# First two chunks loaded, squared, scaled and transposed in halves on two queues, with products of zeros on TensorE until they come

## The chip, the cores and the metric

The kernel runs on one core of a Trainium2 chip. The metric is the device time of one execution in microseconds (us). Five engines run their own instruction queues in order: TensorE (PE; its weight loads are shown as PEld), VectorE (DVE), ScalarE (ACT), GpSimd (POOL) and SyncE (SP). DMAs are issued from SP's queue and from ACT's queue; in the profile they are DMA queues q1 (SP) and q10 (ACT).

## What is computed

The reference is one step of a two-layer decoder trunk: a retention layer and a sliding-window attention layer, over a prompt of 1024 tokens and 8 single decode tokens. Only the start of the first layer matters here:

```
h = rmsnorm(x, g_norm)          # x: 1024 prompt rows and 8 decode rows, 1024 wide
proj = h @ w_in                 # q, k, v, gate
```

where rmsnorm multiplies each row by the inverse root of its mean square (plus 1e-6) and by the gain g_norm. All of it is float32. The kernel forms a product in three passes of rounded float32 (type fp32r): high part times high part, high times low and low times high, where the low part is what the rounding left over.

## The kernel before

The prompt is cut in 8 chunks of 128 rows; chunk 8 stands for the 8 decode rows. For each chunk c there are these steps:

- `xload(c)` issues the load of the chunk (512 KB, 32 KB for chunk 8) on SP's queue.
- `sq(c)` squares it on ACT and sums each row (one Square over 1024 columns, then a read of the accumulator); `pw(c)` makes the factor out of the sum with two small instructions on GpSimd; `sc(c)` multiplies the rows by the factor and the gain `gb` on VectorE.
- `TR(c, b)` transposes the chunk on TensorE in 8 blocks of 128x128, into two PSUM banks; `hi(c, j)` and `lo(c, j)` take the high part (ACT) and the low part (VectorE) of half j out of them. `dcols` puts the columns of the decode rows beside those of the chunks: in the tile of 258 columns, 256 come from two chunks and 2 from the decode rows, so that a product of the first kind needs chunks 0 and 2 and columns of chunk 8.

The weights come in raw tiles of 512 KB (`raw_load`); `w_hi` takes a high part on ACT, `w_lo` a low part on GpSimd or VectorE. The first two weight sets (q0 and k0, head 0) are multiplied in 16 plain slots of 24 products (`plain`, line 556); the work of the other engines in these slots is written out by hand in a list `ops`, and a planner orders everything after them by due times. All queues are in order, so the order in which the program writes instructions of an engine is the order in which the engine takes them.

The start is written out by hand too, at lines 771 to 806: two loads on ACT's queue (the gain `gb`, broadcast to 128 partitions, and the identity `ident`), the table load with a dummy Silu, then on SP's queue chunks 8, 0, 2, two raw tiles of q0, chunks 1 and 3, two raw tiles of k0, chunks 4, 6 and 7. Then

```
    for c in (8, 0, 2):
        sq(c)
        pw(c)
    sc(8)
    ...
    sc(0)
    TR(0, 1)
    dve.tensor_copy(rdec, p8)
    sc(2)
    TR(2, 2)
```

where the lines left out transpose the 8 decode rows into `p8` (8 small transposes on TensorE). After it come `dcols`, `hi`, `lo`, and the high and low parts of the first two weight quarters, A11 and A12.

Of the kernel before, what the change touches and what calls it, by code (L numbers as in the profile page):

```python
# [7 lines left out]
F32 = mybir.dt.float32  # L8
F32R = mybir.dt.float32r
AF = mybir.ActivationFunctionType  # L10
# [4 lines left out]
D = 1024  # L15
# [10 lines left out]
EPS = 1e-6  # L26
# [37 lines left out]
def trunk(tc, x_prompt, x_sample, state_ret, cache_k, cache_v, norm_ret, w_in_ret, ret_out_norm,  # L64
          w_out_ret, norm_swa, w_in_swa, q_norm, k_norm, sinks, w_out_swa, c1, c2,
          y_p, y_s, nrp, nrs, nkp, nvp, nks, nvs):
    nc = tc.nc
    ctx = ExitStack()
    with ctx:
        ctx.enter_context(tc.manual_schedule(engines=MS))  # L70
        _trunk(ctx, tc, nc, locals())


def _trunk(ctx, tc, nc, a):
    x_prompt, x_sample, state_ret = a["x_prompt"], a["x_sample"], a["state_ret"]
# [19 lines left out]
    mm = nc.tensor.matmul  # L95
# [6 lines left out]
    def tr(out, in_, ident, start=True, stop=True):  # L102
        nc.tensor.matmul(out, in_, ident, is_transpose=True, start=start, stop=stop)  # L103
# [13 lines left out]
    def rsq(out, in_, n):  # L117
        nc.gpsimd.tensor_tensor(out, in_, mhalf[:in_.shape[0], :n], ALU.pow)
# [21 lines left out]
    sp = su.enter_context(tc.tile_pool(name="sp", bufs=1, reuse_waits="tile"))  # L140

    xdecr = dcp.tile([128, 8, 40], F32R, name="xdecr")
    xdecd = dcp.tile([128, 4, 40], F32R, name="xdecd")
    oneh_r = dcp.tile([128, 8, 8], F32R, name="oneh_r")
    warm = dcp.tile([1, 8], F32, name="warm")
# [14 lines left out]
    def bank(i, t):  # L160
        return abp.tile([128, 512], F32, tag=f"b{i}{t}", name=f"b{i}{t}")
# [6 lines left out]
    ADD, SUB, MUL = ALU.add, ALU.subtract, ALU.mult  # L168
    act, dve, pool = nc.scalar.activation, nc.vector, nc.gpsimd
# [5 lines left out]
    def raw_tile():  # L175
        return wq.tile([128, 1024], F32, tag="raw", bufs=5, name="raw")

    def raw_load(s, r, eng):

        sub, j = r // 2, r % 2  # L180
        kk = 512 // s.fw
        t = raw_tile().rearrange("p (k f) -> p k f", k=kk)
        r0 = 512 * j + 256 * sub
        eng.dma_start(out=t, in_=w_in_ret[r0:r0 + 128 * kk, s.c0:s.c0 + 2 * s.fw].rearrange("(k p) f -> p k f", p=128))
        s.raw.append(t)
# [224 lines left out]
    gb = sp.tile([128, D], F32, name="gb")  # L410
# [4 lines left out]
    rdif = sp.tile([128, 4, ND], F32, name="rdif")  # L415
    junk = xq.tile([128, D], F32, name="junk")
    X, SS, PO = {}, {}, {}

    def xload(c):
        if c in (0, 1, 2, 3):  # L420
            X[c] = xq.tile([128, D], F32, tag="xq", bufs=4, name="xq")
        elif c == 7:
            X[c] = raw_tile()
        else:
            X[c] = sp.tile([128, D], F32, tag="u", bufs=3, name="u")
        if c == 8:
            X[c] = X[c][0:ND, :]
        nc.sync.dma_start(out=X[c], in_=x_sample[:, 0, :] if c == 8 else x_prompt[0, c * 128:c * 128 + 128, :])

    def sq(c):  # L430
        SS[c] = sp.tile([128, 1], F32, name="ss", bufs=4)
        n = X[c].shape[0]
        act(junk[:n], X[c], AF.Square, accum_out=SS[c][:n])

    def pw(c):
        n = X[c].shape[0]
        pool.tensor_scalar(SS[c][:n], SS[c][:n], 1.0 / D, EPS, MUL, ADD)
        rsq(SS[c][:n], SS[c][:n], 1)

    def sc(c):  # L440
        n = X[c].shape[0]
        dve.scalar_tensor_tensor(X[c], X[c], SS[c][:n], gb[:n], MUL, MUL)

    def TR(c, b):

        PO[c] = [bank(b, j).rearrange("p (k t) -> p k t", k=4) for j in range(2)]
        for j in range(2):
            for k in range(4):
                tr(PO[c][j][:, k, :], X[c][:, 512 * j + k * 128:512 * j + k * 128 + 128], ident)

# [40 lines left out]
    def dcols(t, x, src=None):  # L491

        if src is None:
            k0, r0 = DB[x]
            src = rdec[:, k0:k0 + 4, r0 + 2 * t:r0 + 2 * t + 2]
        h = XH[t][x][:, :, 256:258]
        dve.tensor_copy(h, src)
        dve.tensor_tensor(XL[t][x][:, :, 256:258], src, h.bitcast(F32), SUB)
# [81 lines left out]
    def prod_slot(s, j, t):  # L580
# [14 lines left out]
        if j >= 3:  # L595
# [10 lines left out]
    ops = [  # L606
        [o(w_hi, q0, "A21", 0), o(w_hi, q0, "A22", 0), o(keep, 0, 0), o(keep, 0, 1), o(w_lo, q0, "A21", 0, pool),
         o(w_lo, q0, "A22", 0), o(xload, 5), o(sq, 1), o(pw, 1)],
        [o(sq, 3), o(pw, 3), o(w_hi, k0, "A11", 0), o(w_hi, k0, "A12", 0), o(sc, 1), o(keep, 2, 0), o(keep, 2, 1),
         o(w_lo, k0, "A11", 0, pool), o(w_lo, k0, "A12", 0)],  # L610
        [o(hi, 1, 0), o(hi, 1, 1), o(w_hi, k0, "A21", 0), o(w_hi, k0, "A22", 0), o(sc, 3), o(dcols, 0, T3), o(lo, 1, 0),
         o(lo, 1, 1), o(w_lo, k0, "A21", 0, pool), o(w_lo, k0, "A22", 0)],
        [o(hi, 3, 0), o(hi, 3, 1), o(sq, 4), o(t12, 1), o(dcols, 0, B22), o(lo, 3, 0), o(lo, 3, 1), o(pw, 4), o(t34, 1)],
        [o(sq, 6), o(th, T2, 1), o(t12, 3), o(sc, 4), o(pw, 6), o(t34, 3), o(rsums)],
        [o(th, T2, 3), o(th, T1, 1), o(sc, 6), o(dcols, 1, B11), o(dcols, 1, B21), o(tl, T2, 1), o(tl, T2, 3)],
        [o(hi, 4, 0), o(hi, 4, 1), o(lo, 4, 0), o(lo, 4, 1), o(sq, 5), o(pw, 5), o(keep, 4, 0), o(keep, 4, 1),
# [14 lines left out]
    n = 0  # L631
# [32 lines left out]
    for s in sets[2:]:  # L664
# [31 lines left out]
        for r in range(2 * s.subs):  # L696
            free = raws[-5] + 1.6
            need = min(reads[r])
            t = max(free, need - 13.0)
            t = raw_t[0] = max(t, raw_t[0] + 0.01)  # L700
# [4 lines left out]
        if v:  # L705
            n = len(slots)
# [64 lines left out]
    dve.memset(warm, 0.0)  # L771
    pool.memset(xdecr.bitcast(F32), 0.0)
    pool.memset(xdecd.bitcast(F32), 0.0)
    nc.scalar.dma_start(out=gb, in_=norm_ret[0].partition_broadcast(128))
    nc.scalar.dma_start(out=ident, in_=a["c1"][:, 0:128])
    act(warm, warm, AF.Silu)
    for c in (8, 0, 2):
        xload(c)
    for r in range(2):
        raw_load(q0, r, nc.sync)  # L780
    for c in (1, 3):
        xload(c)
    for r in range(2):
        raw_load(k0, r, nc.sync)
    for c in (4, 6, 7):
        xload(c)
    for c in (8, 0, 2):
        sq(c)
        pw(c)
    sc(8)  # L790
    p8 = vdp.tile([128, 8, ND], F32, tag="vd", name="pd8")
    for k in range(8):
        tr(p8[:, k, :], X[8][:, k * 128:k * 128 + 128], ident[:ND, :ND])
    sc(0)
    TR(0, 1)
    dve.tensor_copy(rdec, p8)
    sc(2)
    TR(2, 2)
    dcols(0, B11)
    dcols(0, B21)  # L800
    for c, name in ((0, "A11"), (2, "A12")):
# [6 lines left out]
    for n, s in enumerate(slots):  # L808
        while pes and pes[0][0] <= s.t:
            _, fn, args = pes.pop(0)  # L810
# [7 lines left out]
        while ev and ev[0][0] < end:  # L818
            _, _, fn, args = ev.pop(0)
# [25 lines left out]
    def o_view(half):  # L845

        if half:
            return B_hi, B_lo, B_hif
        return [t.rearrange("p a b -> p (a b)").rearrange("p (k t) -> p k t", k=16) for t in (A_hi, A_lo, A_hif)]
# [291 lines left out]
    O_hi, O_lo, _ = o_view(0)  # L1141
# [550 lines left out]
    def so_all():  # L1692
        order = [(ft, ti) for ti in range(3) for ft in range(6)] + [(ft, ti) for ft in (6, 7) for ti in range(3)]
        early = []

        def start(ft, ti):
            so_ahead(ft // 2 + 1)
            t0, t1 = TG[ti]
            n = t1 - t0
            xr = iop2.tile([128, 384], F32, tag="xr", bufs=2, name="xr2")  # L1700
            nc.sync.dma_start(out=xr[:, :n], in_=xscr[ft, :, t0:t1])
            nso[0] += 1
            ps = (msp.tile([128, 512], F32, tag="ms", name="pm") if nso[0] % 3 == 0 else
                  pjp.tile([128, 512], F32, tag="pj", name="pj"))
            for k in range(7):
                proj(ps[:, :n], so_slots[ft // 2], ft % 2, t0, t1, first=(k == 0), last=False, ks=[k])
                yield 3 * n / 2400.0
            early.append((ft, ti, ps, xr))

        def finish():  # L1710
            ft, ti, ps, xr = early.pop(0)
            t0, t1 = TG[ti]
            n = t1 - t0
            proj(ps[:, :n], so_slots[ft // 2], ft % 2, t0, t1, first=False, last=True, ks=[7])
            yield 3 * n / 2400.0
            yt = io("sq", 2)
            nc.vector.tensor_tensor(yt[:, :n], ps[:, :n], xr[:, :n], ALU.add)
            if pend_y:
                so_y(*pend_y.pop(0))
            pend_y.append((ft, ti, yt))  # L1720

        for ft, ti in order:
            while early and (oready[early[0][1]] or len(early) == 3):
                while not oready[early[0][1]]:
                    yield 1e9
                yield from finish()
            while ti == 2 and not oready[2]:
                yield 1e9
            yield from start(ft, ti)
        while early:  # L1730
            yield from finish()
        while pend_y:
            so_y(*pend_y.pop(0))
# [43 lines left out]
    out = so_all()  # L1777
# [85 lines left out]
```

## Time and profile before

| | |
|---|---|
| median of 3 runs | 1357.28 us (1355.23 to 1359.15) |
| the profiled execution's own time | 1359.16 us |
| its span, first to last instruction | 1357.4 us |
| mean granted clock of TensorE | 0.989 |
| TensorE busy | 1313.8 us, 97% of the span |
| GpSimd, VectorE, ACT busy | 56%, 55%, 49% |

Times inside the trace are counted from the span's start. A line such as L442 is the source line of the kernel; many steps share a helper's line, so the tile's name tells them apart: u is chunk 8 here (and later chunks), xq are chunks 0 to 3, ss the row sums, xh and xl the high and low parts of chunks, woh and wol those of weights, raw the weight tiles, pd the transposed decode rows, b the PSUM banks. In rows of instructions the first number is the start, the second the time to the end of the last of the merged instructions, and brackets hold the idle time of the engine before it and what ended it. The granted clock (PEclk) is a share of 2.4 GHz.

### The profile page before, as it was taken

What the parts mean: (1) busy time and instruction counts of PE and PEld (TensorE: products, weight loads), DVE (VectorE), ACT (ScalarE), POOL (GpSimd) and SP (SyncE); (2) the same over time, 40 slices, a digit from 0 to 9 for tenths busy, and PEclk for the clock granted to TensorE, in tenths of its full rate; (3) what the DMA queues carried; (4) which work ended last, traced back from release to release, by engine and by line L of the source; (5) the groups of instructions that cost most, each with busy time, mean ns of one, the idle gap of its engine ahead of it and who ended that gap; (6) DMA issues with size and microseconds to landing.
All of it is one profiled execution on the core that took longest, in us unless ns stands there. A gap on an engine that the chain in (4) does not pass through costs nothing.

```text
span 1357.4 us, 25979 instructions
## 1 busy us (share of the span) xinstructions
PE 1313.8 (97%) x9541; PEld 1252.9 (92%) x9541; DVE 744.6 (55%) x1436; ACT 670.8 (49%) x1692; POOL 759.8 (56%) x886
## 2 busy tenths in 40 slices
PE   6999999999999999898989999999999999999998
PEld 6999999999999999787868889988999999998998
DVE  6943665656565653577762112334567777779321
ACT  5532555555565663576751111244576766667311
POOL 6753656656566663698976554563376666544000
PEclk9999999999999999999999999998999999999999
DMA  6314767677676762556546444451111111113533
GB/s 220 103 55 141 216 206 238 164 236 231 183 236 187 229 180 63 194 179 208 173 149 185 145 144 125 142 169 55 32 49 46 48 44 47 34 34 97 166 83 81
DMA packets 193859, 187.19 MB, mean 138 GB/s; under 512 B 12756, under 2 KB 173580, under 8 KB 193716
## 3 DMA queue, kind: packets, MB, share of 16 engines
q1 hardware_dynamic: 156832, 148.34, 35.8%
q10 hardware_dynamic: 36900, 37.19, 8.6%
q8 instruction: 75, 1.23, 0.4%
q14 instruction: 52, 0.43, 0.1%
HBM read 129.11 MB, written 57.41 MB: 137 GB/s over the span
## 4 chain that ended last, share of the span: by engine, by line
PE 84%; DVE 6%; POOL 3%; ACT 3%; DMA 2%; issue 2%; ACTq 0%; SPq 0%; POOLq 0%; DVEq 0%
PE b L340 7%; PE b L342 7%; PE b L341 7%; PE pj L1111 5%; PE pj L1112 5%; PE pj L1113 5%; PE pj L1160 4%; PE pj L1161 4%; PE pj L1162 4%; PE b L334 4%; PE b L333 4%; PE b L335 4%; PE tr L103 4%; PE S L922 1%; PE S L923 1%
## 5 line engine op out<-in xcount | busy, mean ns | idle before, releaser
L340 PE MATMUL b<-xh,woh 128*128 128x258 f32 x784 | 222.4, 284 | 0.0
L342 PE MATMUL b<-xh,wol 128*128 128x258 f32 x784 | 221.9, 283 | 0.0
L341 PE MATMUL b<-xl,woh 128*128 128x258 f32 x784 | 221.6, 283 | 0.0
L1111 PE MATMUL pj<-A_hi,wh 128*128 128x384 f32 (+1 forms) x512 | 173.0, 338 | 1.9 <-ACT Qd L1416 1.9
L1113 PE MATMUL pj<-A_hi,wl 128*128 128x384 f32 (+1 forms) x512 | 166.2, 325 | 0.0
L1112 PE MATMUL pj<-A_lo,wh 128*128 128x384 f32 (+1 forms) x512 | 166.2, 325 | 0.0
L1101 POOL TENSOR_TENSOR wl<-wr,wh 128x512 fp32r<-128x512 f32 (+1 forms) x68 | 124.6, 1844 | 50.5 <-DVE wh L1100 21.2
L340 PEld LDWEIGHTS b<-xh,woh 128*128 128x128 f32 x784 | 148.2, 189 | 1.2
L341 PEld LDWEIGHTS b<-xl,woh 128*128 128x128 f32 x784 | 148.8, 190 | 0.0
L342 PEld LDWEIGHTS b<-xh,wol 128*128 128x128 f32 x784 | 148.2, 189 | 0.0
L334 PE MATMUL b<-wol,xh 128*128 128x256 f32 x448 | 126.1, 282 | 1.2 <-DVE wol L224 1.2
L333 PE MATMUL b<-woh,xh 128*128 128x256 f32 x448 | 125.9, 281 | 0.0
L335 PE MATMUL b<-woh,xl 128*128 128x256 f32 x448 | 125.8, 281 | 0.0
L1527 POOL TENSOR_TENSOR s<-s,sm 128x512 f32<-128x512 f32 x64 | 67.6, 1058 | 76.5 <-DVE sm L1526 71.4
L282 POOL TENSOR_TENSOR yl<-yd,yh 128x256 fp32r<-128x256 f32 x64 | 56.3, 880 | 82.6 <-PE od L289 39.0
L1111 PEld LDWEIGHTS pj<-A_hi,wh 128*128 128x128 f32 x512 | 98.0, 191 | 2.4 <-ACT Qd L1416 2.2
L1112 PEld LDWEIGHTS pj<-A_lo,wh 128*128 128x128 f32 x512 | 98.0, 191 | 0.0
L1113 PEld LDWEIGHTS pj<-A_hi,wl 128*128 128x128 f32 x512 | 97.8, 191 | 0.0
L224 POOL TENSOR_TENSOR wol<-raw,woh 128x512 fp32r<-128x512 f32 x52 | 68.8, 1330 | 48.0 <-ACT woh L219 47.2
L334 PEld LDWEIGHTS b<-wol,xh 128*128 128x128 f32 x448 | 84.4, 188 | 1.4 <-DVE wol L224 1.4
L333 PEld LDWEIGHTS b<-woh,xh 128*128 128x128 f32 x448 | 84.4, 188 | 0.7
L335 PEld LDWEIGHTS b<-woh,xl 128*128 128x128 f32 x448 | 84.4, 188 | 0.0
(384 smaller groups left out, 3836.4 us busy)
## 6 DMA issues: line engine op xcount, KB each, us to landing
raw<-in_w_in_ret_dram ACTq DMA_DIRECT2D x44, 512.0 KB
st<-in_state_ret_dram SPq DMA_DIRECT2D x64, 256.0 KB
out_dram<-st SPq DMA_DIRECT2D x64, 256.0 KB
wr<-in_w_out_ret_dram SPq DMA_DIRECT2D x32, 512.0 KB
wr<-in_w_in_swa_dram SPq DMA_DIRECT2D x18, 512.0 KB
vb<-vscr SPq DMA_DIRECT2D x64, 128.0 KB
evp<-qks SPq DMA_DIRECT2D x32, 256.0 KB
evw<-gsc SPq DMA_DIRECT2D x32, 256.0 KB
```

The lines of the kernel that those rows point to most:

```text
L224: eng.tensor_tensor(lo, src_of(s, name, sub), hi.bitcast(F32), SUB)
L333: mm(dst, xh, wh, start=a and i == 0, stop=False, skip_group_check=True)
L334: mm(dst, xh, wl, start=False, stop=False, skip_group_check=True)
L335: mm(dst, xl, wh, start=False, stop=z, skip_group_check=True)
L340: mm(dst, wh, xh, start=a, stop=False, **sg)
L341: mm(dst, wh, xl, start=False, stop=False, **sg)
L342: mm(dst, wl, xh, start=False, stop=z, **sg)
L1101: lo_eng[0].tensor_tensor(lo[:, js, :], raw[:, i:i + step, :], hi.bitcast(F32)[:, js, :], ALU.subtract)
L1111: mm(ps, hi[:, k, fs], xh[:, k, t0:t1], start=first and k == ks[0], stop=False)
L1112: mm(ps, hi[:, k, fs], xl[:, k, t0:t1], start=False, stop=False)
L1113: mm(ps, lo[:, k, fs], xh[:, k, t0:t1], start=False, stop=last and k == ks[-1])
L1527: nc.gpsimd.tensor_tensor(st[:, :, 0:256], st[:, :, 0:256], sm.unsqueeze(2).broadcast_to([128, 2, 256]), ALU.mult)
```

## The change

On SP and ACT both: chunks 0 and 2 are loaded in two halves of 512 columns, one on each queue, ahead of all else; chunk 8 is loaded behind chunks 0 and 2 and the two raw tiles of q0. Squares of chunks 0 and 2 are taken by halves with a scaled input, so that their sums add up to the mean; their scalings are split in halves too, each followed by its four transposes. The order of Squares is 0, 2, 8 instead of 8, 0, 2, and that of scalings 0, 8, 2 instead of 8, 0, 2. The dummy Silu with its table load stands behind the DMA issues. 34 products of a zeroed tile with itself, of 320 columns, are put ahead on TensorE; their result in bank (0, 0) is never read.

```
     def xload(c):
...
-        nc.sync.dma_start(out=X[c], in_=x_sample[:, 0, :] if c == 8 else x_prompt[0, c * 128:c * 128 + 128, :])
+        if c in FIRST:
+            for j in range(2):
+                js = slice(512 * j, 512 * j + 512)
+                (nc.sync, nc.scalar)[j].dma_start(out=X[c][:, js], in_=x_prompt[0, c * 128:c * 128 + 128, js])
+        else:
+            nc.sync.dma_start(out=X[c], in_=x_sample[:, 0, :] if c == 8 else x_prompt[0, c * 128:c * 128 + 128, :])
 
     def sq(c):
-        SS[c] = sp.tile([128, 1], F32, name="ss", bufs=4)
+        SS[c] = sp.tile([128, 2], F32, name="ss", bufs=4)
         n = X[c].shape[0]
-        act(junk[:n], X[c], AF.Square, accum_out=SS[c][:n])
+        if c in FIRST:
+            for j in range(2):
+                js = slice(512 * j, 512 * j + 512)
+                act(junk[:, js], X[c][:, js], AF.Square, scale=D ** -0.5, accum_out=SS[c][:, j:j + 1])
+        else:
+            act(junk[:n], X[c], AF.Square, accum_out=SS[c][:n, 0:1])
 
     def pw(c):
         n = X[c].shape[0]
-        pool.tensor_scalar(SS[c][:n], SS[c][:n], 1.0 / D, EPS, MUL, ADD)
-        rsq(SS[c][:n], SS[c][:n], 1)
+        r_ = SS[c][:n, 0:1]
+        if c in FIRST:
+            pool.tensor_scalar(r_, r_, SS[c][:, 1:2], EPS, ADD, ADD)
+        else:
+            pool.tensor_scalar(r_, r_, 1.0 / D, EPS, MUL, ADD)
+        rsq(r_, r_, 1)
...
+    def scTR(c, b):
         for j in range(2):
+            xj = X[c][:, 512 * j:512 * j + 512]
+            dve.scalar_tensor_tensor(xj, xj, SS[c][:, 0:1], gb[:, 512 * j:512 * j + 512], MUL, MUL)
+            TR(c, b, (j,))
+
+    def TR(c, b, js=(0, 1)):
+        if 0 in js:
+            PO[c] = [bank(b, j).rearrange("p (k t) -> p k t", k=4) for j in range(2)]
+        for j in js:
             for k in range(4):
                 tr(PO[c][j][:, k, :], X[c][:, 512 * j + k * 128:512 * j + k * 128 + 128], ident)
...
+    xload(0)
     nc.scalar.dma_start(out=gb, in_=norm_ret[0].partition_broadcast(128))
     nc.scalar.dma_start(out=ident, in_=a["c1"][:, 0:128])
-    act(warm, warm, AF.Silu)
-    for c in (8, 0, 2):
-        xload(c)
+    xload(2)
     for r in range(2):
         raw_load(q0, r, nc.sync)
-    for c in (1, 3):
+    for c in (8, 1, 3):
         xload(c)
     for r in range(2):
         raw_load(k0, r, nc.sync)
     for c in (4, 6, 7):
         xload(c)
-    for c in (8, 0, 2):
+    act(warm, warm, AF.Silu)
+
+    zb = bank(0, 0)
+    for _ in range(34):
+        mm(zb[0:40, 0:320], xdecr[:, 0, :], xdecr.rearrange("p a b -> p (a b)"), start=True, stop=True)
+    for c in (0, 2, 8):
         sq(c)
         pw(c)
+    scTR(0, 1)
     sc(8)
     p8 = vdp.tile([128, 8, ND], F32, tag="vd", name="pd8")
     for k in range(8):
         tr(p8[:, k, :], X[8][:, k * 128:k * 128 + 128], ident[:ND, :ND])
-    sc(0)
-    TR(0, 1)
+    scTR(2, 2)
     dve.tensor_copy(rdec, p8)
-    sc(2)
-    TR(2, 2)
     dcols(0, B11)
     dcols(0, B21)
```

## Rows read from the trace of the kernel before

**Rows 1.** The page, busy time and share of the span of each engine.
```profile
PE 1313.8 (97%) x9541; PEld 1252.9 (92%) x9541; DVE 744.6 (55%) x1436; ACT 670.8 (49%) x1692; POOL 759.8 (56%) x886
```
**Rows 2.** Waits, 0 to 45 us: engine, line, waited for, us in total, times, longest.
```profile
PE b L556 <- POOL wol L224: 1.5, 1, 1.5
```
**Rows 3.** Chain that ended last, 0 to 60 us: start, length, what.
```profile
1.19 5.50 DMA xq<-in_x_prompt_dram
...
15.43 3.79 POOL wol L224 x3
...
25.63 1.72 PE b L556 x12
```
**Rows 4.** A stretch: length; PE, PEld, DVE, ACT, POOL busy; clock, DMA, GB/s.
```profile
100.00:545.00 445.00, 445.00 (x3726) 440.38 (x3725) 249.22 (x418) 229.38 (x522) 253.49 (x299) 1.00 0.64 193
```
**Rows 5.** Instructions in order of time, 0 to 15 us, of several queues.
```profile
0.72 0.36 POOL L772 MEMSET xdecr<- 128x320 f32 x1 [0.29 <-POOLq L1846]
0.72 0.40 SPq L428 DMA_DIRECT2D u<-in_x_sample_dram  x1
3.08 1.04 ACT L433 ACTIVATE junk<-u 8x1024 f32<-8x1024 f32 x1
4.56 0.55 POOL L118 TENSOR_TENSOR ss<-ss,mhalf 8x1 f32<-8x1 f32 x1
5.33 1.27 DVE L442 SCALAR_TENSOR_TENSOR u<-u,ss,gb 8x1024 f32<-8x1024 f32 x1 [4.42 <-DMA gb<-in_norm_ret_dram]
7.47 0.99 PE L103 MATMUL pd<-ident,u 8*128 8x8 f32 x8 [7.47 <-DMA ident<-const_c_dram]
8.53 1.06 ACT L433 ACTIVATE junk<-xq 128x1024 f32<-128x1024 f32 x1 [0.60 <-DMA xq<-in_x_prompt_dram]
12.23 1.57 PEld L103 LDWEIGHTS b<-ident,xq 128*128 128x128 f32 x8 [0.44 <-DVE xq L442]
13.39 0.60 ACT L459 ACTIVATE xh<-b 128x512 fp32r<-128x512 f32 x1
14.24 0.60 ACT L459 ACTIVATE xh<-b 128x512 fp32r<-128x512 f32 x1 [0.25 <-PE b L103]
```
**Rows 6.** DMA: all queues, 1.5 to 2.0 us; then the queue of ACT, 2.0 to 3.0.
```profile
DMA packets 25, 0.07 MB, mean 139 GB/s; under 512 B 8, under 2 KB 8, under 8 KB 25
...
q10 hardware_dynamic: 68, 0.28, 90.5%
```
**Rows 7.** DMA packets in the half microseconds from 8.0, 10.0 and 10.5 us.
```profile
DMA packets 196, 0.19 MB, mean 389 GB/s; under 512 B 6, under 2 KB 196, under 8 KB 196
...
DMA packets 96, 0.19 MB, mean 373 GB/s; under 512 B 7, under 2 KB 65, under 8 KB 96
...
DMA packets 58, 0.20 MB, mean 410 GB/s; under 512 B 2, under 2 KB 10, under 8 KB 58
```
**Rows 8.** First products; without a start ahead: ns min/median/max, first and last start.
```profile
14.04 0.93 PEld L556 LDWEIGHTS b<-xh,woh 128*128 128x128 f32 x4 [0.24 <-ACT xh L459]
20.25 1.12 PE L556 MATMUL b<-xl,woh 128*128 128x258 f32 x8
...
L556 PE MATMUL b<-xh,woh x4: 419/420/583, 14.0 to 14.8; 128*128 128x258 f32 x4
...
L556 PE MATMUL b<-xh,wol x7: 281/283/304, 16.4 to 17.1; 128*128 128x258 f32 x7
```
**Rows 9.** Two later idle stretches of TensorE, and the granted clock behind them.
```profile
634.67 1.09 PE L103 MATMUL tr<-ident,on 128*128 128x128 f32 x4 [3.75 <-DVE on L975]
...
634.00:636.00 2.00, 1.33 (x7) 1.36 (x8) 1.12 (x3) 1.35 (x4) 2.00 (x2) 0.52 0.58 218
...
712.69 0.79 PE L1162 MATMUL tr<-A_hi,wl 128*128 128x512 f32 x1 [3.28 <-POOL wl L1101]
...
713.00:716.00 3.00, 3.00 (x8) 2.32 (x8) 0.02 (x1) 0.00 (x0) 1.96 (x1) 0.50 0.66 209
716.00:718.00 2.00, 2.00 (x10) 1.61 (x9) 0.68 (x1) 0.00 (x0) 1.19 (x1) 1.00 0.83 262
```

More of the change, by code (lines that the diff above doesn't have):

```diff
@@ L417, in _trunk @@
     X, SS, PO = {}, {}, {}
+    FIRST = (0, 2)
     def xload(c):
@@ L427, in xload @@
             X[c] = X[c][0:ND, :]
-        nc.sync.dma_start(out=X[c], in_=x_sample[:, 0, :] if c == 8 else x_prompt[0, c * 128:c * 128 + 128, :])
+        if c in FIRST:
[4 more added lines that the diff above has]
+            nc.sync.dma_start(out=X[c], in_=x_sample[:, 0, :] if c == 8 else x_prompt[0, c * 128:c * 128 + 128, :])
     def sq(c):
-        SS[c] = sp.tile([128, 1], F32, name="ss", bufs=4)
+        SS[c] = sp.tile([128, 2], F32, name="ss", bufs=4)
         n = X[c].shape[0]
-        act(junk[:n], X[c], AF.Square, accum_out=SS[c][:n])
+        if c in FIRST:
[4 more added lines that the diff above has]
+            act(junk[:n], X[c], AF.Square, accum_out=SS[c][:n, 0:1])
     def pw(c):
         n = X[c].shape[0]
-        pool.tensor_scalar(SS[c][:n], SS[c][:n], 1.0 / D, EPS, MUL, ADD)
-        rsq(SS[c][:n], SS[c][:n], 1)
+        r_ = SS[c][:n, 0:1]
[4 more added lines that the diff above has]
+        rsq(r_, r_, 1)
     def sc(c):
         n = X[c].shape[0]
-        dve.scalar_tensor_tensor(X[c], X[c], SS[c][:n], gb[:n], MUL, MUL)
-    def TR(c, b):
-        PO[c] = [bank(b, j).rearrange("p (k t) -> p k t", k=4) for j in range(2)]
+        dve.scalar_tensor_tensor(X[c], X[c], SS[c][:n, 0:1], gb[:n], MUL, MUL)
+    def scTR(c, b):
         for j in range(2):
+            xj = X[c][:, 512 * j:512 * j + 512]
[5 more added lines that the diff above has]
+        for j in js:
             for k in range(4):
```

## Prediction, made before the changed kernel was run

> **What bounds the kernel now.** I read the page's table of engines first: TensorE is busy 97% of the span [rows 1], so a change is worth what it takes off or adds to TensorE's idle time. The waits of TensorE in the first 45 us came next: it idles 7.5 us before its first instruction [rows 5], waits between the parts of the start, and later once more, 1.5 us for a weight's low part on GpSimd [rows 2]. Last, the chain of work that ended last, from 0 to 60 us [rows 3]: it starts with the load of chunk 0, passes Square, power, scaling and the transposes, and then lies on GpSimd, whose subtractions for the low parts take most of the time from 15.43 us until TensorE goes on at 25.63 us. Further on, from 100 to 545 us, TensorE is busy for the whole of the stretch [rows 4]. The queues are in order and keep their order, so whatever the start is delayed by, the end is delayed by nearly as much. Everything the diff touches lies ahead of these points. The number to work out is when GpSimd's run now at 15.43 us starts, and when TensorE's first products do, which now start at 14.04 us [rows 8].
>
> **How large the stake is.** Medians 0.3% apart (4.07 us) are about what a measurement of this kernel can tell from no change. All of the start before the first product is 14 us, some 7 of it waiting for data.
>
> **The change, part by part.**
>
> *Chunk 0 comes earlier.* Now its load is issued at 1.19 us as SP's second and is waited for until 6.7 [rows 3]. From 2.0 to 3.0 us the other queue, with the broadcast of the gain, has the DMA engines almost to itself [rows 6]. After the change both halves are first in their queues: 0.5 MB at 280 to 410 GB/s [rows 6, 7] is 1.3 to 1.9 us from about 1.6 us on, plus 0.5 us until an engine sees it (from 8.0 us on all packets are small ones, so chunk 2's are out, and its Square starts at 8.53 [rows 5, 7]): 4 us, at most 5.5. Two half Squares cost 2 x 0.60 us by ACT's half-width row instead of 1.06, and one more read of the accumulator, 1.6 at most; the power about 0.85 as now; halves of the scaling 0.64 each (half of 1.27) [rows 5]. The gain lands later than now, behind up to 1.6 MB, at 6 to 8 us. So chunk 0 is scaled by 9 us and transposed by 10 or so, some 2 us earlier than now.
>
> *The eight decode rows come later, and this decides.* Now they are SP's first load, issued at 0.72 us, squared at 3.08 [rows 5]. In the diff the load of chunk 8 moves behind chunks 0 and 2 and both weight tiles of q0 on SP. Ahead of it are then the same bytes that now precede the end of the second weight tile: four tiles of 0.5 MB, the gain and the identity. Splitting or interleaving them changes no sum. Those weight tiles are the 1 KB packets: all packets from 8.0 to 8.5 us, 58 of 96 from 10.0 to 10.5 (65 under 2 KB less 7 under 512 B), 8 of 58 after that [rows 7]. So the engines are through with them between about 9.5 and 10.6 us. With 0.5 us until it is seen, the rows land at 10.0 to 11.1 us. I take 10.4, since the first loads should waste a little less at the start than now.
>
> The Trainium skill, "DMA: Bandwidth & Descriptors", section "Why a DMA increments its semaphore by 16 and not by 1", bears on this: a transfer from SP uses as many of the 16 engines as divide its row count, so 8 rows use 8 engines, and the eight need not wait for the slowest of sixteen. By that rule the rows would land near the lower bound, 10.0, and the sum below would be 0.4 us smaller. The trace agrees as far as it goes: this load shows as 16 packets, eight of them under 512 B [rows 6].
>
> *What is queued behind that landing.* ACT's order is now Square of 0, 2, 8, then the high parts of chunk 0; so all of ACT's high parts wait for chunk 8's Square. VectorE's order is scaling of 0, of 8, then of 2; TensorE's is transposes of 0, of 8, of 2. So chunk 2 waits for chunk 8 on two engines, which it doesn't have to wait for now (8 was finished by 6.6 us on VectorE). From 10.4 us, by the present rows [rows 5]: from the start of Square to the end of the power 2.03 (3.08 to 5.11), issue 0.04, scaling 1.27: 13.74. Half scalings of chunk 2 end at 14.38 and 15.02. On TensorE the eight small transposes take 0.99 at the present rate: 14.8, since they come ahead of chunk 2. From chunk 2's first transpose to its first high part is 1.16 us now (12.23 to 13.39): 15.96 against 13.39, which is **2.6 us later**. The second high part, the high part of A12 and GpSimd's run at 15.43 follow at their present distances.
>
> *The products of zeros, and the clock.* 34 products of 320 columns start once GpSimd's memset is done, at about 1.1 us [rows 5]. A 258-column product is issued every 0.23 us at the lower rate and every 0.12 at the full one (four weight loads in 0.93 us at 14.04, seven starts from 16.4 to 17.1 [rows 8]); by columns that is 0.285 and 0.15 us. The rate now rises at about 16 us: products of 420 ns before, of 283 after [rows 8]. The granted clock reads 1.00 throughout there, so I go by the durations, which are those of 1.2 and 2.4 GHz. At 712.69 us work resumes after an idle stretch and the clock is back at 716, 3.3 us later [rows 9]; at the start it took some 4 us from chunk 2's transposes at 12.23 to 16. So, with a rise 3 to 6 us after 1.1 to be safe, the zeros end at 7.7 to 9.2 us; if the rate never rises, at 10.8. In each case that is before chunk 8 is scaled, and costs nothing.
> But what they warm cools again: after chunk 0's transposes TensorE has nothing to do from about 10 us to 13.8, nearly 4 us. After idle stretches of 3.75 and 3.28 us the granted clock was at 0.5, 1.2 GHz, when work resumed [rows 9]; the 1.45 us at 24.2 did not show it [rows 2]. If the clock holds, the transposes take half as long and chunk 2's halves are set by their scaling: of the 1.16 us some 0.5 fall away, 0.7 stay, and the second high part comes at 15.02 + 0.7 = 15.7 against 14.24. Then the shift is **1.5 us**. If it falls, the products meet the lower rate for up to 3 us more from 16.6 on, 13 instead of 8 of them, which adds up to 0.6 us.
>
> *The rest costs nothing:* the table load of 1.3 us moves behind four DMA issues of about 0.4 us each on ACT (as SP's [rows 5]) and ends by about 4 us, under chunk 0's load (uncovered, it would cost at most those 1.3 us). Wider accumulators and the power of two halves add one read of a column. Chunk 2's second half, behind the gain on ACT's queue, lands by 8 to 9 us, before chunk 8. Loads of chunks 1 and 3 move back by 32 KB.
>
> *The sum.* Shift between 1.5 and 3.2 us; with 10.0 to 11.1 for the landing, 1.1 to 3.9. TensorE's clock most likely falls: I take +2.4 us. The profiled execution took 1359.16 us (span 1357.4 plus 1.8 around it), so 1361.6 in its own time. It lay 1.9 above the median of the runs shown; against that median, 1357.28 + 2.4 = **1359.7 us**, 0.18% slower, within 0.3%.
>
> **Rivals.**
>
> *The eight rows come early* (the short transfer passes the weight tiles): then chunk 2's second half on ACT's queue is last, at 7 to 8 us. Square of that half 0.8, Square to power of 8 2.07, scaling 1.27 + 0.64, transposes 0.7: the first high part at 12.5 to 13.5 against 13.39, so 0.1 us slower to 0.9 faster, 1356.4 to 1357.4. For it: small loads elsewhere are fast (issued 0.72, squared 3.08). Against it: that one had an empty queue. Chance 0.15.
>
> *The change does what it says*: chunks 0 and 2 set the first products, chunk 8 doesn't. With its second half there at 7.5, Square 0.8, power 0.9, half a scaling 0.64 and fast transposes 0.7 bring the first high part to 10.6 instead of 13.39, 2.8 us ahead; with eight products at the full rate 3.7 us, 1353.6. It needs chunk 8 out of VectorE's and ACT's order, which the code does not do. Chance 0.04. This is at the edge of 0.3%.
>
> *Slower by over 0.3%: cold products.* If TensorE stays at 1.2 GHz through the first two slots, 48 products at 0.23 us run from 16.6 to 27.6, where they end at 21.4 now [rows 8]: 6.2 us later, 1363.5. It decides from a rate that rises later than about 23 us (23 - 16.6 is 27 slow products, the other 21 take 2.5), some 9 us after work resumes, beyond the times seen (3.3, and at most 4 to 6 at the start). A landing at 11.3 or later with a fallen clock gives the same. Chance 0.12.
>
> **Numbers.** Forecast (1.1 to 3.9 us slower, 1358.4 to 1361.2) 0.69, rivals 0.15, 0.04, 0.12. The medians of runs shown differ by up to 2 us by themselves, so the range is 1355.4 to 1362.2. Over 0.3% slower takes rival three: 0.12, plus 0.01 from the forecast's upper end; over 0.3% faster half of rival two, 0.02; within 0.3% 0.85.
>
> **What the profile after would show.** Right: Square of 8x1024 on ACT starts at 10 to 11 us behind a wait of some microseconds for the x_sample load; scaling of chunk 8 on VectorE at 12.4; a gap of about 4 us on TensorE ahead of the small transposes, and behind it 1.1 us or more from chunk 2's first transpose to its first high part; GpSimd's run of low parts starting at 17 to 18.1 us. Wrong: Square of chunk 8 before 9 us, or the first real product before 14 us. If the shift is there at 20 us and gone at 60, a slack that I do not see took it.

## The result and the profile after

The median of ten runs after is 1360.52 us (1357.36 to 1365.07), of ten runs before 1356.9 us: +3.6 us, a ratio of 1.0030 with a 95% interval of 1.0017 to 1.0044, that is 2.3 to 6.0 us. The forecast was 1359.7 us, 2.4 slower; the sign and the cause came as forecast, the size was 1.2 us short. The medians alone could not show that shortfall, since 2.4 lies inside their interval; the marks in the trace below, at +3.7 us, do. The interval reaches past 0.3%, so on which side of that line the true value lies is not settled. The profiled execution after took 1365.07 us (span 1363.2), more than its median, at a mean granted clock of 0.982 against 0.989 before; its span is 5.8 us longer than before (1357.4), some 2 us of that from behind the stretch that the change touches, so the argument below goes by marks early in the trace.

The page, busy time of each engine, against [rows 1]:

```profile
PE 1322.9 (97%) x9575; PEld 1258.9 (92%) x9575; DVE 744.3 (55%) x1438; ACT 671.0 (49%) x1696; POOL 763.9 (56%) x886
```

TensorE has the 34 products of zeros more. The chain that ended last, 0 to 20 us (start, length, what), against [rows 3]:

```profile
0.72 3.65 DMA xq<-in_x_prompt_dram
4.39 7.12 DMA u<-in_x_sample_dram
11.59 1.16 ACT junk L445 x2
...
13.67 1.28 DVE u L458
15.00 1.02 PE pd L103 x8
16.01 1.91 PE b L103 x8
```

The second piece is the answer. Before, the chain ran through chunk 0 and then GpSimd; now it runs through `u`, which is chunk 8, the eight decode rows. They are issued at 4.39 us and come in 7.12 us later; their Square, factor, scaling and transposes follow on the chain, and the transposes of chunk 2 (`b`, 16.01) behind those.

Instructions after, a selection in order of time, of ACT, VectorE, TensorE and GpSimd, as [rows 5, 8]:

```profile
1.14 6.86 PE L814 MATMUL b<-xdecr 128*40 128x320 f32 x34 [1.14 <-POOL xdecr L796]
4.31 0.61 ACT L443 ACTIVATE junk<-xq 128x512 f32<-128x512 f32 x1
7.81 1.41 DVE L464 SCALAR_TENSOR_TENSOR xq<-xq,ss,gb 128x512 f32<-128x512 f32 x2 [6.90 <-DMA gb<-in_norm_ret_dram]
8.61 1.32 PE L103 MATMUL b<-ident,xq 128*128 128x128 f32 x8 [0.62 <-DVE xq L464]
9.76 0.63 ACT L443 ACTIVATE junk<-xq 128x512 f32<-128x512 f32 x1 [2.31 <-DMA xq<-in_x_prompt_dram]
11.59 1.05 ACT L445 ACTIVATE junk<-u 8x1024 f32<-8x1024 f32 x1 [1.11 <-DMA u<-in_x_sample_dram]
13.67 1.27 DVE L458 SCALAR_TENSOR_TENSOR u<-u,ss,gb 8x1024 f32<-8x1024 f32 x1 [4.45 <-POOL ss L118]
15.00 1.02 PE L103 MATMUL pd<-ident,u 8*128 8x8 f32 x8 [5.06 <-DVE u L458]
15.95 1.97 PE L103 MATMUL b<-ident,xq 128*128 128x128 f32 x8
17.09 0.60 ACT L483 ACTIVATE xh<-b 128x512 fp32r<-128x512 f32 x1 [2.88 <-PE b L103]
17.75 2.60 PE L580 MATMUL b<-xh,woh 128*128 128x258 f32 x8
19.14 3.77 POOL L224 TENSOR_TENSOR wol<-raw,woh 128x512 fp32r<-128x512 f32 x3 [1.74 <-ACT woh L219]
22.88 1.13 PE L580 MATMUL b<-xh,woh 128*128 128x258 f32 x8
29.33 0.75 PE L580 MATMUL b<-xh,wol 128*128 128x258 f32 x4 [1.06 <-POOL wol L224]
```

Read it in pairs with the rows of before. Chunk 0's Square starts at 4.31 instead of 6.78, and its transposes end at 9.9 instead of 12.2: the head start is there, although the scaling has to wait for the gain until 7.81 (8.88 before). Then the brackets: ACT waits for `u`, VectorE 4.45 us for its factor, TensorE 5.06 us for its scaling. Chunk 2's first high part comes at 17.09 instead of 13.39 (+3.70), the first products at 17.75 instead of 14.04 (+3.71), GpSimd's run of low parts at 19.14 instead of 15.43 (+3.71), TensorE's wait for it ends at 29.33 instead of 25.63 (+3.70).

A mark further on, the first of the stores of v (min/median/max ns, first and last start), before:

```profile
L718 SPq DMA_DIRECT2D vscr<-evw x4: 290/292/358, 117.4 to 381.3; - x4
```

and after:

```profile
L742 SPq DMA_DIRECT2D vscr<-evw x4: 291/294/360, 121.1 to 385.8; - x4
```

117.4 became 121.1: +3.7 once more, and the median moved by 3.6. All experiments below are read at this mark and at GpSimd's run too, because single runs of one kernel lie up to 10 us apart (1364.9 to 1375.0 in one of them).

The clock in the same stretch of after, columns as [rows 4]:

```profile
9.00:11.00 2.00, 0.93 (x7) 0.45 (x5) 0.22 (x1) 0.72 (x2) 0.33 (x2) 1.00 1.16 349
11.00:13.00 2.00, 0.00 (x0) 0.00 (x0) 0.00 (x0) 1.41 (x3) 0.72 (x2) 0.69 0.98 384
13.00:15.00 2.00, 0.00 (x1) 0.01 (x1) 1.33 (x2) 1.21 (x3) 1.26 (x3) 0.50 1.05 356
...
19.00:21.00 2.00, 1.88 (x8) 1.89 (x9) 2.00 (x5) 2.00 (x5) 1.86 (x2) 0.50 1.04 414
21.00:23.00 2.00, 2.00 (x15) 2.00 (x15) 0.50 (x1) 0.14 (x2) 1.91 (x2) 0.75 0.26 98
23.00:25.00 2.00, 2.00 (x19) 2.00 (x18) 1.14 (x1) 1.93 (x5) 1.15 (x3) 1.00 0.23 66
```

TensorE does nothing from 9.9 to 15.0 us. Within that gap the granted clock drops from 2.4 to 1.2 GHz (0.69 is a mean of the two), and it is back near 22 us (0.75 from 21 to 23 us is again a mean), some 7 us after work resumed.

### The profile page after: what moved, and what is told of

Its sections match the earlier page's. It is cut to its first block, busy times and chain, and to the rows that moved or that the text cites. A ratio compares the mean times of both kernels' runs of the same rounds, so it can differ in the third digit from the quotient of the medians.

```text
span 1363.2 us, 26057 instructions
## 1 busy us (share of the span) xinstructions
PE 1322.9 (97%) x9575; PEld 1258.9 (92%) x9575; DVE 744.3 (55%) x1438; ACT 671.0 (49%) x1696; POOL 763.9 (56%) x886
## 4 chain that ended last, share of the span: by engine, by line
PE 82%; DVE 6%; DMA 4%; POOL 3%; ACT 3%; issue 2%; ACTq 0%; POOLq 0%; DVEq 0%
PE b L340 6%; PE b L342 6%; PE b L341 6%; PE pj L1137 5%; PE pj L1139 5%; PE pj L1138 5%; PE b L334 4%; PE b L333 4%; PE b L335 4%; PE tr L103 4%; PE pj L1186 4%; PE pj L1187 3%; PE pj L1188 3%; PE S L948 1%; PE S L949 1%
```

## Experiments

My theory: chunk 8's late landing, together with its place in the order ahead of chunk 2, sets the start; the delay goes into the end one for one; the zeros neither help nor cost; the clock lost in the gap is worth about 1 us. The rivals, in words: the load's place alone explains everything; halves and queues are worth 2 us or more once chunk 8 is out of the way; the zeros themselves help or cost; the lost clock costs nothing, or most of the shift; some slack behind the start absorbs a delay.

**Only the load of chunk 8 back at the head.** The new order of Squares, scalings and transposes stays.

```
+    xload(8)
     xload(0)
...
-    for c in (8, 1, 3):
+    for c in (1, 3):
```

> The changed kernel with only the load of the 8 decode rows moved back to the head of SP's queue; the order of Squares (0, 2, 8) and scalings stays. Theory A (the order of the instructions behind chunk 8 counts as much as its landing): Square of 8x1024 then follows chunk 2's second half, which was squared at 9.76 us, so it starts at 10.5 instead of 11.6; the first products at about 16.6 instead of 17.75, and the time is 1.1 us below the changed kernel, 2.5 above the kernel before. Rival B (the late landing alone is the cause): nearly all of the 3.6 us comes back, and the time is within 0.5 us of the kernel before.

Measured: 1360.92 against 1357.23 us, ratio 1.0027 (1.0014 to 1.0040); first store of v at 120.1. Its instructions:

```profile
9.84 0.63 ACT L443 ACTIVATE junk<-xq 128x512 f32<-128x512 f32 x1 [1.12 <-DMA xq<-in_x_prompt_dram]
10.59 1.05 ACT L445 ACTIVATE junk<-u 8x1024 f32<-8x1024 f32 x1
...
18.15 3.81 POOL L224 TENSOR_TENSOR wol<-raw,woh 128x512 fp32r<-128x512 f32 x3 [1.74 <-ACT woh L219]
```

The Square of `u` has no bracket now: its data are long there, and it only stands behind chunk 2's second half in ACT's order. GpSimd's run starts at 18.15, 1.0 us earlier than after and 2.72 later than before. The late load costs 1.0 us more than an early one in this order. The other 2.7 us stay with the order, in which chunk 2's second half, squared only at 9.84, now stands ahead of chunk 8; how the 2.7 us divide between the two this run does not show. So the load's place alone does not explain the shift. The medians (+3.7 us, interval 1.9 to 5.4) are too coarse to tell 2.7 from 3.7.

**Load and order of chunk 8 both undone.** What is left of the change are halves, two queues and zeros.

```
+    xload(8)
     xload(0)
...
-    for c in (0, 2, 8):
+    for c in (8, 0, 2):
         sq(c)
         pw(c)
-    scTR(0, 1)
     sc(8)
     ... transposes of chunk 8 ...
+    scTR(0, 1)
     scTR(2, 2)
```

> The changed kernel with the load of chunk 8 first and with the order of Squares and of scalings as before the change (8, 0, 2); halves, two queues and the products of zeros stay. Theory A: chunk 2's second half, seen at 9.8 us behind the gain on ACT's queue, now sets the start: Square 0.8, power 0.95, half scaling 0.7, transposes 0.5 to 1.0, first high part at 13.0 to 13.5 against 13.39 before the change: the whole 3.6 us comes back and not more than 0.5 us beyond. Rival B expects the same as for the load alone. Rival C (the halves and two queues gain what they were meant to, once chunk 8 is out of the way): 2 us or more below the kernel before.

Measured: 1358.84 against 1357.23 us, ratio 1.0007 (0.9996 to 1.0018); first store of v at 117.4, as before.

```profile
9.03 0.63 ACT L443 ACTIVATE junk<-xq 128x512 f32<-128x512 f32 x1 [0.57 <-DMA xq<-in_x_prompt_dram]
...
14.14 2.49 PE L580 MATMUL b<-xh,woh 128*128 128x258 f32 x8
...
15.42 3.77 POOL L224 TENSOR_TENSOR wol<-raw,woh 128x512 fp32r<-128x512 f32 x3 [1.46 <-ACT woh L219]
```

15.42 against 15.43 [rows 3]: the whole shift is gone, and nothing is won. So all 3.7 us hang on where chunk 8 stands in loads and order, and halves on two queues give nothing here: chunk 2's second half, on ACT's queue behind the gain and the identity, is squared at 9.03, where the whole chunk was squared from 8.53 [rows 5].

**Without the zeros.** The 34 products are left out, the rest is as after.

```
-    zb = bank(0, 0)
-    for _ in range(34):
-        mm(zb[0:40, 0:320], ...)
```

> The changed kernel without the 34 products of zeros. Theory A: their clock is lost in the 5 us of idling ahead of chunk 8's transposes, so nothing changes: within 0.5 us of the changed kernel, and transposes of chunk 0 take about 0.25 us each instead of 0.13, off the path. Rival D (the zeros cost something, by the clock or by power): 1 us or more faster than the changed kernel. Rival E (they help): 1 us or more slower.

Measured: 1361.45 against 1357.23 us, ratio 1.0026 (1.0013 to 1.0039); products at 17.64, first store of v at 121.0.

```profile
19.04 3.78 POOL L224 TENSOR_TENSOR wol<-raw,woh 128x512 fp32r<-128x512 f32 x3 [1.75 <-ACT woh L219]
```

All within 0.11 us of after: the zeros neither help nor cost. Chunk 0's transposes are slower without them (1.94 instead of 1.32 us), but off the path; chunk 2's take 1.97 us with them and without, since the gap loses what they won.

**32 more products of zeros in the gap**, behind chunk 0's transposes.

```
     scTR(0, 1)
+    for _ in range(32):
+        mm(zb[0:40, 0:320], ...)
     sc(8)
```

> The changed kernel with 32 more products of zeros behind chunk 0's transposes, to fill the idle stretch up to chunk 8's transposes (5.1 us, 32 x 0.15 = 4.8). Theory A: granted clock 1.00 through the first products, transposes 273 ns instead of 421; the second high part of chunk 2 then waits for its scaling alone, some 0.9 us earlier; first products at about 17.0, time 0.9 us below the changed kernel, 2.7 above the kernel before. Rival F (the clock is most of the loss): 2.5 us or more below the changed kernel.

Measured: 1360.17 against 1357.23 us, ratio 1.0021 (1.0008 to 1.0034); first store of v at 120.2. Its windows and two instructions:

```profile
11.00:13.00 2.00, 2.00 (x16) 1.57 (x14) 0.00 (x0) 1.40 (x3) 0.74 (x2) 1.00 1.01 393
13.00:15.00 2.00, 1.55 (x11) 0.96 (x9) 1.32 (x2) 1.22 (x3) 1.26 (x3) 1.00 1.05 357
```

```profile
15.67 1.32 PE L103 MATMUL b<-ident,xq 128*128 128x128 f32 x8
...
18.21 3.79 POOL L224 TENSOR_TENSOR wol<-raw,woh 128x512 fp32r<-128x512 f32 x3 [0.81 <-ACT woh L219]
```

The clock holds at 1.00, chunk 2's eight transposes take 1.32 instead of 1.97 us, and GpSimd's run starts 0.93 us earlier than after (19.14 to 18.21). The first products start at 17.58 and not at the 17.0 expected, because by the trace they wait for VectorE's rounding of chunk 8's columns. The clock lost in the gap is worth 0.9 us in the trace; the other 2.8 us stay with chunk 8.

**Chunk 8 still later**, behind chunks 1 and 3 and both raw tiles of k0.

```
-    for c in (8, 1, 3):
+    for c in (1, 3):
...
-    for c in (4, 6, 7):
+    for c in (8, 4, 6, 7):
```

> The changed kernel with the load of chunk 8 put off further, behind chunks 1 and 3 and both weight tiles of k0 (2.1 MB more on SP's queue, about 5.4 us at 0.39 MB per us). Theory A: Square of 8x1024 starts at about 17 us, GpSimd's run at about 24.5, and the time is about 9 us above the kernel before, 5.4 above the changed one: a delay of chunk 8 goes into the end one for one. Rival G (the start is slack, and the 3 us come from somewhere else): no more than 2 us above the changed kernel.

Measured: 1368.38 against 1356.59 us, ratio 1.0091 (1.0067 to 1.0114); first store of v at 126.8.

```profile
17.23 1.05 ACT L445 ACTIVATE junk<-u 8x1024 f32<-8x1024 f32 x1 [6.67 <-DMA u<-in_x_sample_dram]
...
24.78 3.79 POOL L224 TENSOR_TENSOR wol<-raw,woh 128x512 fp32r<-128x512 f32 x3 [1.74 <-ACT woh L219]
```

Against after, the Square of `u` moves by 5.64 us, GpSimd's run by 5.64, the store of v by 5.7. No slack takes any of it. The median moved by 11.8 us where the marks stand 9.4 later than before; the interval for the time, 9.1 to 15.5 us, holds 9.4.

**Chunk 8 last.** Loads as after, but chunk 2 does not wait for chunk 8: Squares of 0 and 2, chunk 0's high parts and A11's are put ahead of chunk 8's Square, its scaling and transposes behind chunk 2's, with 10 and 12 zeros in TensorE's gaps.

```
-    for c in (0, 2, 8):
+    for c in (0, 2):
         sq(c)
         pw(c)
     scTR(0, 1)
+    ... 10 zeros ...
+    scTR(2, 2)
+    ... 12 zeros ...
+    for j in range(2):
+        hi(0, j)
+    w_hi(q0, "A11", 0)
+    sq(8)
+    pw(8)
     sc(8)
     ... transposes of chunk 8 ...
-    scTR(2, 2)
```

> The changed kernel's loads, chunk 8 late as there, but chunk 2 does not wait for chunk 8: Squares 0, 2, then high parts of chunk 0, then Square of 8; scalings and transposes 0, 2, 8; 10 and 12 products of zeros behind the transposes of chunks 0 and 2 hold the clock. Theory A: chunk 8 is scaled at 13.7 us as before, but chunk 2 has been done by 13; GpSimd's run starts at about 15 instead of 19.1, the first products (which need chunk 8's columns) at about 16 instead of 17.75: 1 to 2 us above the kernel before, that is, half or more of the loss was the order behind chunk 8 and not its landing. Rival B (the landing alone): 3 us or more above the kernel before.

Measured: 1365.22 against 1356.59 us, ratio 1.0068 (1.0042 to 1.0093); first store of v at 124.6. This was a miss. The trace of the start says why:

```profile
13.10 1.26 ACT L483 ACTIVATE xh<-b 128x512 fp32r<-128x512 f32 x2
...
13.89 4.95 POOL L224 TENSOR_TENSOR wol<-raw,woh 128x512 fp32r<-128x512 f32 x4
13.95 5.97 DVE L458 SCALAR_TENSOR_TENSOR u<-u,ss,gb 8x1024 f32<-8x1024 f32 x1 [0.93 <-POOL ss L118]
18.93 1.05 POOL L453 TENSOR_SCALAR ss<-ss 128x1 f32<-128x1 f32 x1
...
21.59 2.06 PE L580 MATMUL b<-xh,woh 128*128 128x258 f32 x8 [0.62 <-DVE xh L521]
```

Chunk 2's high parts do come early, at 13.10 instead of 17.09, and GpSimd starts its low parts at 13.89. But VectorE's scaling of chunk 8, issued 0.06 us later, takes 5.97 us instead of 1.27: it ends 1.08 us after GpSimd's four subtractions, and GpSimd's next small instruction, of 0.18 us elsewhere, takes 1.05 while the scaling runs. The products need columns of chunk 8, so they start at 21.59. The run shows this collision, and nothing about what the order alone is worth. A late chunk 8 that chunk 2 does not wait for was not seen without that collision; the first experiment undoes the load alone, the second load and order together.

**Two attempts at a faster kernel.** The first has chunk 8's load and order as before, both halves of chunk 2 on SP, and 6 + 6 zeros in TensorE's gaps. The second is the kernel before with zeros alone, 34 ahead and 8 behind the transposes of chunk 8.

```
-    (nc.sync, nc.scalar)[j].dma_start(...)
+    (nc.sync, nc.scalar if c == 0 else nc.sync)[j].dma_start(...)
...
+    for _ in range(6):
+        mm(zb[0:40, 0:320], ...)
     scTR(0, 1)
+    for _ in range(6):
+        mm(zb[0:40, 0:320], ...)
     scTR(2, 2)
```

> The kernel with chunk 8 first in loads, Squares and scalings, halves of chunk 0 on two queues, but both halves of chunk 2 on SP's queue (not behind the gain and the identity on ACT's), and 6 products of zeros each behind chunk 8's and chunk 0's transposes, so that the clock holds. Theory A: chunk 2 is seen at about 8.3 us instead of 9.0, transposes take 273 ns, GpSimd's run of low parts starts at 14.0 to 14.6 instead of 15.4, and the time is about 1 us below the kernel before. Rival C (halves bring nothing, whatever the order): no start earlier than 15.4.

> The kernel before with nothing of the change but the products of zeros, 34 at the start and 8 behind chunk 8's transposes. Theory A: chunk 0 and 2 are transposed at 273 ns instead of 421, the first products start at about 13.2 instead of 14.04 us, and GpSimd's run at about 14.6 instead of 15.43: about 0.8 us faster than before. Rival F (the clock is worth more): 2 us or more.

Measured: the first 1358.69 against 1356.59 us, ratio 1.0020 (1.0005 to 1.0035); the second 1355.89 against 1356.59, ratio 0.9994 (0.9981 to 1.0006). GpSimd's run in the first:

```profile
14.24 3.79 POOL L224 TENSOR_TENSOR wol<-raw,woh 128x512 fp32r<-128x512 f32 x3 [0.61 <-ACT woh L219]
```

and in the second:

```profile
14.65 3.79 POOL L224 TENSOR_TENSOR wol<-raw,woh 128x512 fp32r<-128x512 f32 x3 [0.72 <-ACT woh L219]
```

That is 1.2 and 0.8 us ahead of before, and the first store of v stands as far ahead (116.2 and 116.6). For the first the time says otherwise, so both were run again.

> The kernel of e5 once more, unchanged: its trace showed GpSimd's run and the first store of v 1.2 us earlier than before the change, its time 2.7 us above. If the time follows the trace: 0 to 2 us below the kernel before. If something further on costs what the start gains: again 1 to 4 us above, and the marks of the trace (first store of v, last store of the decode stage, first load of the next stage) fall back behind those of before somewhere after 120 us.

> The kernel before with products of zeros alone, once more and on the same chip as e9: 0.5 to 1 us below the kernel before by its trace (first store of v at 116.6 instead of 117.4). If a spread of 2 us between chips or phases of the clock hides such sizes, it may come out on either side.

Measured: 1356.97 against 1357.75 us, ratio 1.0002 (0.9988 to 1.0015), and 1356.18 against 1357.75, ratio 0.9998 (0.9984 to 1.0011). The first result did not repeat. Both kernels start earlier in the trace, in the second round too: GpSimd's run at 14.24 and 14.66, the first store of v at 116.2 and 116.7. That either is faster in time is not shown. A gain of about 1 us is smaller than these intervals, and in the second round's traces it is no longer there at the last store of v (381.2 and 381.3, before 381.3), where the first round's had 380.1 and 381.1. From the first store of v to the last the twelve traces take 263.9 to 265.0 us, so one trace cannot tell whether something absorbs 1 us there.

## Why the prediction was right, and where its size was off

*What waits for chunk 8: right.* ACT's high parts, VectorE's scaling of chunk 2 and TensorE's transposes of chunk 2 all stood behind it. With its order and load undone the shift is 0; with its load later by 5.64 us everything is later by that.

*The landing: this step was mis-sized.* The prediction took 10.4 us, within 10.0 to 11.1, from "the engines are through with them between about 9.5 and 10.6 us" and "the first loads should waste a little less at the start than now". The rows landed at 11.51 (4.39 + 7.12 in the chain). Of the 1.1 us, 0.7 lie in the choice of 10.4 out of its own range, whose upper end was 11.1, and 0.4 lie beyond that end. It had also held that "Splitting or interleaving them changes no sum": the sum of the bytes stayed, the rate at which they moved did not. The bytes moved in the first 11 us, by windows (last column GB/s), before:

```profile
1.00:3.00 2.00, 0.00 (x0) 0.00 (x0) 0.00 (x0) 1.32 (x2) 0.25 (x2) 1.00 0.55 174
3.00:5.00 2.00, 0.00 (x0) 0.00 (x0) 0.00 (x0) 1.21 (x3) 0.62 (x2) 1.00 0.90 282
5.00:7.00 2.00, 0.00 (x0) 0.00 (x0) 1.27 (x1) 0.22 (x1) 0.11 (x1) 1.00 0.98 326
```

and after:

```profile
1.00:3.00 2.00, 1.86 (x7) 1.30 (x8) 0.00 (x0) 0.10 (x1) 0.25 (x2) 1.00 0.51 114
3.00:5.00 2.00, 2.00 (x9) 1.39 (x8) 0.00 (x0) 1.99 (x5) 0.00 (x0) 1.00 0.99 336
5.00:7.00 2.00, 2.00 (x16) 1.54 (x15) 0.00 (x0) 0.90 (x4) 0.89 (x2) 1.00 0.91 258
```

From 1 to 7 us that is 1.56 MB before (2 us times 174 + 282 + 326) and 1.42 MB after, and from 7 to 11 us another 1.52 against 1.45 MB (381 and 381, 378 and 349 GB/s): 0.22 MB less, or 0.6 us at some 370 GB/s. The packets under 2 KB, less those under 512 B, are those of the weight tiles, and they end later than before, where 58 were left in the half microsecond from 10.0 us and 8 from 10.5 [rows 7]. After, there are 111 from 10.0 us, 27 from 10.5 and 2 from 11.0; the last two of these half microseconds:

```profile
DMA packets 59, 0.13 MB, mean 260 GB/s; under 512 B 7, under 2 KB 34, under 8 KB 59
...
DMA packets 38, 0.15 MB, mean 291 GB/s; under 512 B 1, under 2 KB 3, under 8 KB 38
```

The prediction's 0.5 us from the last of these packets to the wait's end then gives the measured 11.5. The other runs narrow down which edit made the first loads slower. From 1 to 11 us 2.87 MB move after, 2.84 without the zeros, but 3.00 in the first two experiments, where chunk 8's load is back at the head and halves and queues are as after; before it was 3.09. So over half of the loss goes with taking chunk 8's load off the head, and leaving out the zeros does not give it back. Why is open: the trace after shows that SP issued nothing for 1.5 us ahead of chunk 8's load, and whether that gap moved the landing was not tried.

The Trainium skill, "DMA: Bandwidth & Descriptors", section "Why a DMA increments its semaphore by 16 and not by 1", was named beside the lower bound: eight rows use eight engines. The trace does not bear out that they gain by it behind other loads: they landed at 11.5 us, after the weight tiles' last packets, and 10.0 would have been further off.

*From the landing to the high part: right.* From the Square's start to chunk 2's first high part it took 5.50 us (11.59 to 17.09); the prediction's terms add up to 5.56 (10.40 to 15.96). With the measured landing the same terms give +3.7. The forecast of 2.4 lay 0.2 below its own 2.6 for a fallen clock, which makes up the rest of the shortfall.

*The clock: fell, as taken.* A held clock was priced at 1.1 us (2.6 less 1.5); with the gap filled it was 0.9. It came back later than assumed, near 22 us: 16 products of the first slot ran at the lower rate instead of 13. At the second slot, which before began so,

```profile
18.33 1.12 PE L556 MATMUL b<-xh,woh 128*128 128x258 f32 x8
```

TensorE was 4.55 us behind (18.33 to 22.88 us), 0.84 more than at the first; at 29.33 it was 3.70 again, since there GpSimd's run ends its wait. So the "up to 0.6 us" for slow products was real at the second slot and nothing at the end, where GpSimd covers it.

*Costed at nothing: right.* Zeros ended at 8.0 us (7.7 to 9.2 was forecast) and their removal changed nothing. The gain was there at 7.8 us (6 to 8), chunk 0's transposes ended at 9.9 ("by 10 or so"). Chunk 2's second half was squared at 9.76, later than the 8 to 9 given for its landing; with chunk 8 landing still later that had no price, but in the first experiment it was the end of ACT's wait.

*The carry: right, one for one,* by the marks at 19, 29 and 121 us and the run with chunk 8 still later; the median, with its interval of 2.3 to 6.0 us, agrees.

*The rivals.* That the rows come early falls with the Square at 11.59. That the change does what it says falls too. Of cold products as the cause of more than 0.3%: the late clock alone did not reach the 23 us that it needed, but its other condition, a landing at 11.3 us or later with a fallen clock, was met. The price was 3.7 us, 0.27%, just short of the 4.07 that it was said to give: on this rival the forecast of "within 0.3%" held by a narrow margin, and partly by luck. Its 6.2 us were also read at the end of the slow products; TensorE's wait of 1.45 us ahead of 25.63 would have covered part of them.

## What to carry to other kernels

Before moving a load back, ask in how many engines' orders its consumers stand ahead of others: 32 KB of decode rows held up ACT, VectorE and TensorE at once; undoing the load alone gave back 1.0 of 3.7 us, load and order together all of it. Add a small load's landing from the measured drain of all that is ahead of it on its queue, and do not count on a rearrangement of the first loads to keep their rate: here it fell. A stage that starts earlier gains nothing if its successor needs a second input that now comes later. Products of zeros held the clock here when they reached up to the real work, and were worth nothing when a gap of 5.1 us followed them.

## What was not expected of the hardware

VectorE and GpSimd shut each other out, and for longer than one instruction: the scaling of 8x1024 took 5.97 us instead of 1.27 behind four GpSimd subtractions in a row (4.95 us), as if it had to wait for all four. The Trainium skill, "SBUF — State Buffer", section "Who interferes with whom", says that an operation of VectorE with two inputs from SBUF contends with one of GpSimd that reads SBUF, that the pair of ports they share is an exclusive lock, and that the order of issue decides who blocks. The trace agrees: GpSimd was first by 0.06 us and VectorE waited; and it did not get its turn between two of the four instructions. The kernel after shows it the other way about:

```profile
14.29 3.11 POOL L224 TENSOR_TENSOR wol<-raw,woh 128x512 fp32r<-128x512 f32 x1 [0.66 <-ACT woh L219]
...
14.87 1.40 DVE L464 SCALAR_TENSOR_TENSOR xq<-xq,ss,gb 128x512 f32<-128x512 f32 x2
```

The subtraction takes 1.27 and 1.30 us in the two attempts at a faster kernel. Here VectorE's scalings lie without a break from 13.67 to 16.27, and it ends 1.13 us after the last of them, at 17.40.
